# Average pooling over groups of four: rows of 126 KB per partition instead of blocks of 64 KB

## The chip, the cores and the metric

The kernel runs on one core of one Trainium2 chip. The metric is the device time of one execution in microseconds (us); lower is better. A core has compute engines with queues of their own (of these VectorE and ScalarE work here), SyncE, which only issues transfers, and 16 DMA engines that move all data between memory and the on-chip buffer of 128 partitions.

## The reference

The input is 64 x 256 x 8192 floats (536.87 MB), the output 64 x 256 x 2048 floats (134.22 MB). Each output is the mean of four neighbours, and the windows do not overlap:

```python
out_len = (length - kernel_size) // stride + 1     # kernel_size = stride = 4
for i in range(out_len):
    start = i * stride
    output[:, :, i] = np.mean(x[:, :, start : start + kernel_size], axis=2)
```

Since 8192 is a multiple of four, no window crosses the end of a row. So the input may be taken as one flat array, in which each four neighbours give one output, and cut anywhere at a multiple of four.

## The kernel before, in words

The flat input is cut into 64 blocks of 128 x 16,384 floats (8 MB). Within a block partition p holds the p-th run of 16,384 floats (64 KB), so a block is one contiguous piece of memory. The outputs of a block are 128 runs of 4096 floats (16 KB).

Every block goes through four steps. `load` (L44) is one DMA that SyncE issues, into one of two input buffers `xt` of 64 KB per partition. `sums` is two additions on VectorE: the first (L50) adds even and odd elements and writes the 8192 sums into the first half of the same input buffer, the second (L54) adds neighbours of these and writes 4096 sums into the result buffer `r`. `scale` (L59) multiplies by a quarter on ScalarE, in place in `r`. A store then writes the results to memory.

Results are gathered for two blocks (a group): `r` holds 2 x 4096 floats per partition and there are two such buffers. In the first four groups (`SINGLES` counts blocks here, 8) each block is scaled and stored by itself, from ScalarE's queue (L75, 2 MB). In the 26 groups after that the two blocks are scaled in one instruction and stored in one DMA (L78, 4 MB); in memory these are two runs of 16 KB per partition, 2 MB apart (`both`).

At the end stand block 62, loaded and stored alone, and block 63, loaded and computed in two pieces of 10,240 and 6144 floats per partition (`LAST`). The last whole group (blocks 60 and 61) is scaled after the loads of the end were issued, and it and all later results are stored from SyncE's queue (L87, L90, L95), behind the loads.

The order of the work follows from the queues and the buffers. SyncE issues the load of block i+2 once VectorE has finished both additions of block i, because they use the same input buffer. DMAs issued by SyncE go into one queue (q1 in the profile) and those of ScalarE into another (q10); the 16 DMA engines serve both. VectorE and ScalarE work in program order. VectorE's second addition needs a free result buffer, that is, the store of two groups earlier must have landed.

Of the kernel before, what the change touches and what calls it, by code (L numbers as in the profile page):

```python
# [1 line left out]

# [4 lines left out]


RUN = 16384

SINGLES = 8
LAST = (10240, 6144)


@with_exitstack
def kernel(
    ctx: ExitStack,
    tc: tile.TileContext,
    x: bass.AP,
    kernel_size: bass.AP,  # L20
    stride: bass.AP,
    out: bass.AP,
):
    nc = tc.nc
    K, S = int(kernel_size), int(stride)
    assert K == S == 4
    B, C, L = x.shape
    P = nc.NUM_PARTITIONS
    dt = x.dtype
    M = RUN // K  # L30
    blocks = B * C * L // (P * RUN)
    assert blocks * P * RUN == B * C * L and L % K == 0 and blocks % 2 == 0
    assert sum(LAST) == RUN

    xb = x.rearrange("b c l -> (b c l)").rearrange("(n p m) -> n p m", p=P, m=RUN)
    ob = out.rearrange("b c l -> (b c l)").rearrange("(n p m) -> n p m", p=P, m=M)

    pin = ctx.enter_context(tc.tile_pool(name="xin", bufs=2))
    pout = ctx.enter_context(tc.tile_pool(name="res", bufs=2))

    def load(i, a=0, b=RUN, xt=None):
        if xt is None:
            xt = pin.tile([P, RUN], dt, name="xt")
        nc.sync.dma_start(out=xt[:, a:b], in_=xb[i][:, a:b])  # L44
        return xt

    def sums(o, xt, a=0, b=RUN):
        v = xt[:, a:b].rearrange("p (m k) -> p m k", k=2)
        h = xt[:, a : (a + b) // 2]
        nc.vector.tensor_tensor(  # L50
            out=h, in0=v[:, :, 0], in1=v[:, :, 1], op=mybir.AluOpType.add
        )
        w = h.rearrange("p (m k) -> p m k", k=2)
        nc.vector.tensor_tensor(  # L54
            out=o, in0=w[:, :, 0], in1=w[:, :, 1], op=mybir.AluOpType.add
        )

    def scale(o):
        nc.scalar.mul(o, o, 1.0 / K)  # L59

    def edges(cuts):
        at = [sum(cuts[:j]) for j in range(len(cuts) + 1)]
        return list(zip(at[:-1], at[1:]))

    def both(i):
        return ob[i : i + 2].rearrange("n p m -> p n m")

    for i in range(0, blocks - 2, 2):
        r = pout.tile([P, 2, M], dt, name="r")
        for h in range(2):  # L70
            xt = load(i + h)
            sums(r[:, h, :], xt)
            if i < SINGLES:
                scale(r[:, h, :])
                nc.scalar.dma_start(out=ob[i + h], in_=r[:, h, :])  # L75
        if SINGLES <= i < blocks - 4:
            scale(r[:])
            nc.scalar.dma_start(out=both(i), in_=r[:])  # L78

    n = blocks - 1  # L80
    t = pout.tile([P, 2, M], dt, name="r")
    xt = load(n - 1)
    xl = None
    for a, b in edges(LAST):
        xl = load(n, a, b, xl)
    scale(r[:])
    nc.sync.dma_start(out=both(n - 3), in_=r[:])  # L87
    sums(t[:, 0, :], xt)
    scale(t[:, 0, :])
    nc.sync.dma_start(out=ob[n - 1], in_=t[:, 0, :])  # L90
    for a, b in edges(LAST):
        o = t[:, 1, a // K : b // K]
        sums(o, xl, a, b)
        scale(o)
        nc.sync.dma_start(out=ob[n][:, a // K : b // K], in_=o)  # L95


# [1 line left out]
_INS = ['x', 'kernel_size', 'stride']  # L99
_OUTS = [((64, 256, 2048), 'float32')]  # L100

_NUMBERS = {'kernel_size': 4, 'stride': 4}


# [26 lines left out]
```

## Time and profile before

| What | Value |
|---|---|
| median of 3 runs | 1554.46 us (1554.44 to 1555.88) |
| profiled execution: time | 1554.4 us |
| profiled execution: span | 1552.6 us |
| VectorE busy | 839.7 us (54%) |
| ScalarE busy | 227.4 us (15%) |
| DMA queues q1 and q10 | 81.1% and 18.9% of 16 engines' span |
| first addition, 128 x 8192 | 8692 ns each, 63 of them |
| second addition, 128 x 4096 | 4425 ns each, 63 of them |
| scale, 128 x 8192 and 128 x 4096 | 7029 ns and 3616 ns each |
| loads of 8 MB, issue to landing | 35.1 us (median of 63) |
| stores of 4 MB and 2 MB from ScalarE's queue, issue to landing | 52.0 us and 31.7 us (medians of 26 and 8) |

The span is the time from the first to the last record of the profiled execution; its full time is 1.8 us longer. Busy times are sums over instructions. The two queue rows count the time that packets took; a packet is the piece that one DMA engine moves at a time. A time from issue to landing contains the wait behind other packets of the same engines. The span is also shown in 40 equal slices, with the busy share of each engine in tenths (9 is 90% or more).

### The profile page before, as it was taken

What the parts mean: (1) busy time and instruction counts of PE and PEld (TensorE: products, weight loads), DVE (VectorE), ACT (ScalarE), POOL (GpSimd) and SP (SyncE); (2) the same over time, 40 slices, a digit from 0 to 9 for tenths busy, and PEclk for the clock granted to TensorE, in tenths of its full rate; (3) what the DMA queues carried; (4) which work ended last, traced back from release to release, by engine and by line L of the source; (5) the groups of instructions that cost most, each with busy time, mean ns of one, the idle gap of its engine ahead of it and who ended that gap; (6) DMA issues with size and microseconds to landing.
All of it is one profiled execution on the core that took longest, in us unless ns stands there. A gap on an engine that the chain in (4) does not pass through costs nothing.

```text
span 1552.6 us, 471 instructions
## 1 busy us (share of the span) xinstructions
DVE 839.7 (54%) x130; ACT 227.4 (15%) x39; POOL 0.2 (0%) x4
## 2 busy tenths in 40 slices
DVE  3646556546465464654646546455464554645646
ACT  1111101110111101111011110111101111011111
POOL 0000000000000000000000000000000000000000
DMA  9999999999999999999999999999999999999999
GB/s 417 420 434 438 439 439 439 412 445 444 413 433 435 443 438 439 432 424 429 439 438 433 437 434 419 439 432 438 439 419 434 434 437 439 441 423 442 422 440 400
DMA packets 18292, 671.12 MB, mean 432 GB/s; under 512 B 1649, under 2 KB 1649, under 8 KB 1777
## 3 DMA queue, kind: packets, MB, share of 16 engines
q1 hardware_dynamic: 10064, 545.26, 81.1%
q10 hardware_dynamic: 8224, 125.83, 18.9%
q14 instruction: 4, 0.02, 0.0%
HBM read 536.87 MB, written 134.22 MB: 432 GB/s over the span
## 4 chain that ended last, share of the span: by engine, by line
DMA 71%; DVE 28%; issue 0%; ACT 0%; DVEq 0%
DMA xt<-in_x_dram 71%; DVE xt L50 18%; DVE r L54 9%; ACT r L59 0%; DVEq L54 0%
## 5 line engine op out<-in xcount | busy, mean ns | idle before, releaser
L50 DVE TENSOR_TENSOR xt<-xt 128x8192 f32<-128x8192 f32 (+1 forms) x65 | 556.5, 8561 | 696.1 <-DMA xt<-in_x_dram 696.1
L59 ACT ACTIVATE r<-r 128x8192 f32<-128x8192 f32 (+3 forms) x38 | 226.2, 5951 | 1313.0 <-DVE r L54 1313.0
L54 DVE TENSOR_TENSOR r<-xt 128x4096 f32<-128x4096 f32 (+1 forms) x65 | 283.4, 4360 | 3.9
L59 ACT ACT_TABLE_LOAD x1 | 1.3, 1283 | 0.7 <-PEq L112 0.7
L112 POOL MEMSET const-bfloat16-1.0<- 128x1 bf16 x1 | 0.1, 101 | 0.0
L112 POOL MEMSET const-uint8-127<- 128x1 uint8 x1 | 0.1, 101 | 0.0
L112 POOL MEMSET const-float32-0.0<- 128x1 f32 x1 | 0.1, 98 | 0.2 <-issue 0.2
L112 POOL MEMSET const-float32-1.0<- 128x1 f32 x1 | 0.1, 98 | 0.0
## 6 DMA issues: line engine op xcount, KB each, us to landing
out_dram<-r ACTq DMA_DIRECT2D x26, 4096.0 KB, 52.0
out_dram<-r ACTq DMA_DIRECT2D x8, 2048.0 KB, 31.7
xt<-in_x_dram SPq DMA_DIRECT2D x1, 5120.0 KB, 23.1
out_dram<-r SPq DMA_DIRECT2D x1, 4096.0 KB, 33.0
xt<-in_x_dram SPq DMA_DIRECT2D x1, 3072.0 KB, 30.0
out_dram<-r SPq DMA_DIRECT2D x1, 2048.0 KB, 16.9
out_dram<-r SPq DMA_DIRECT2D x1, 1280.0 KB, 12.9
xt<-in_x_dram SPq DMA_DIRECT2D x63, 35.1
```

What stands on the lines that cost most here:

```text
L50: nc.vector.tensor_tensor(out=h, in0=v[:, :, 0], in1=v[:, :, 1], op=mybir.AluOpType.add)
L54: nc.vector.tensor_tensor(out=o, in0=w[:, :, 0], in1=w[:, :, 1], op=mybir.AluOpType.add)
L59: nc.scalar.mul(o, o, 1.0 / K)
L112: nc = _bacc.Bacc("TRN2", target_bir_lowering=False, num_devices=1)
```

## The change

The cut of the data changes. `RUN` becomes 16,128 floats (63 KB). A group of two halves is now one contiguous piece of memory in which partition p holds 2 x 16,128 floats (126 KB) in a row. The first half of each partition's run is one load and the second half another, so a load takes 63 KB per partition from rows that begin 126 KB apart. The results of a whole group are then one run of 2 x 4032 floats (31.5 KB) per partition.

There are 32 such groups. The first four (`SINGLES` counts groups now, 4) are scaled and stored in halves, 15.75 KB per partition, as before from ScalarE's queue; groups 4 to 30 are scaled and stored whole from ScalarE's queue; the last, group 31, is scaled in halves and stored whole from SyncE's queue. What is left is one contiguous block of 128 x 16,384 floats (`END`), which takes the place of the last block and is loaded, computed and stored in the same two pieces. The single block ahead of it is gone. Input buffers stay at 64 KB per partition; result buffers become 31.5 KB.

```diff
-RUN = 16384
+RUN = 16128
+END = 16384
 
-SINGLES = 8
+SINGLES = 4
 LAST = (10240, 6144)
...
-    xb = x.rearrange("b c l -> (b c l)").rearrange("(n p m) -> n p m", p=P, m=RUN)
-    ob = out.rearrange("b c l -> (b c l)").rearrange("(n p m) -> n p m", p=P, m=M)
+    xf = x.rearrange("b c l -> (b c l)")
+    of = out.rearrange("b c l -> (b c l)")
+    xb = xf[:body].rearrange("(n p h m) -> n p h m", p=P, h=2, m=RUN)
+    ob = of[: body // K].rearrange("(n p m) -> n p m", p=P, m=2 * M)
+    xe = xf[body:].rearrange("(p m) -> p m", p=P)
+    oe = of[body // K :].rearrange("(p m) -> p m", p=P)
...
-    for i in range(0, blocks - 2, 2):
-        r = pout.tile([P, 2, M], dt, name="r")
-        for h in range(2):
-            xt = load(i + h)
-            sums(r[:, h, :], xt)
-            if i < SINGLES:
-                scale(r[:, h, :])
-                nc.scalar.dma_start(out=ob[i + h], in_=r[:, h, :])
-        if SINGLES <= i < blocks - 4:
-            scale(r[:])
-            nc.scalar.dma_start(out=both(i), in_=r[:])
+    for g in range(groups):
+        r = pout.tile([P, 2 * M], dt, name="r")
+        for h in range(2):
+            xt = load(xb[g, :, h, :], 0, RUN)
+            o = r[:, h * M : (h + 1) * M]
+            sums(o, xt, 0, RUN)
+            if g < SINGLES or g == groups - 1:
+                scale(o)
+            if g < SINGLES:
+                nc.scalar.dma_start(out=ob[g][:, h * M : (h + 1) * M], in_=o)
+        if SINGLES <= g < groups - 1:
+            scale(r[:])
+            nc.scalar.dma_start(out=ob[g], in_=r[:])
...
-    n = blocks - 1
-    t = pout.tile([P, 2, M], dt, name="r")
-    xt = load(n - 1)
     xl = None
     for a, b in edges(LAST):
-        xl = load(n, a, b, xl)
-    scale(r[:])
-    nc.sync.dma_start(out=both(n - 3), in_=r[:])
-    sums(t[:, 0, :], xt)
-    scale(t[:, 0, :])
-    nc.sync.dma_start(out=ob[n - 1], in_=t[:, 0, :])
+        xl = load(xe, a, b, xl)
+    nc.sync.dma_start(out=ob[groups - 1], in_=r[:])
+    e = pout.tile([P, 2 * M], dt, name="r")
     for a, b in edges(LAST):
-        o = t[:, 1, a // K : b // K]
+        o = e[:, a // K : b // K]
         sums(o, xl, a, b)
         scale(o)
-        nc.sync.dma_start(out=ob[n][:, a // K : b // K], in_=o)
+        nc.sync.dma_start(out=oe[:, a // K : b // K], in_=o)
```

More of the change, by code (lines that the diff above doesn't have):

```diff
@@ L30, with load, sums @@
     M = RUN // K
-    blocks = B * C * L // (P * RUN)
-    assert blocks * P * RUN == B * C * L and L % K == 0 and blocks % 2 == 0
-    assert sum(LAST) == RUN
-    xb = x.rearrange("b c l -> (b c l)").rearrange("(n p m) -> n p m", p=P, m=RUN)
-    ob = out.rearrange("b c l -> (b c l)").rearrange("(n p m) -> n p m", p=P, m=M)
+    total = B * C * L
+    groups = total // (2 * P * RUN)
+    body = groups * 2 * P * RUN
+    assert L % K == 0 and total - body == P * END
+    assert sum(LAST) == END
+    xf = x.rearrange("b c l -> (b c l)")
[4 more added lines that the diff above has]
+    oe = of[body // K :].rearrange("(p m) -> p m", p=P)
     pin = ctx.enter_context(tc.tile_pool(name="xin", bufs=2))
     pout = ctx.enter_context(tc.tile_pool(name="res", bufs=2))
-    def load(i, a=0, b=RUN, xt=None):
+    def load(src, a, b, xt=None):
         if xt is None:
-            xt = pin.tile([P, RUN], dt, name="xt")
-        nc.sync.dma_start(out=xt[:, a:b], in_=xb[i][:, a:b])
+            xt = pin.tile([P, END], dt, name="xt")
+        nc.sync.dma_start(out=xt[:, a:b], in_=src[:, a:b])
         return xt
-    def sums(o, xt, a=0, b=RUN):
+    def sums(o, xt, a, b):
         v = xt[:, a:b].rearrange("p (m k) -> p m k", k=2)
@@ L63, in edges @@
         return list(zip(at[:-1], at[1:]))
-    def both(i):
-        return ob[i : i + 2].rearrange("n p m -> p n m")
-    for i in range(0, blocks - 2, 2):
-        r = pout.tile([P, 2, M], dt, name="r")
+    for g in range(groups):
+        r = pout.tile([P, 2 * M], dt, name="r")
         for h in range(2):
-            xt = load(i + h)
-            sums(r[:, h, :], xt)
-            if i < SINGLES:
-                scale(r[:, h, :])
-                nc.scalar.dma_start(out=ob[i + h], in_=r[:, h, :])
-        if SINGLES <= i < blocks - 4:
+            xt = load(xb[g, :, h, :], 0, RUN)
[6 more added lines that the diff above has]
+        if SINGLES <= g < groups - 1:
             scale(r[:])
-            nc.scalar.dma_start(out=both(i), in_=r[:])
-    n = blocks - 1
-    t = pout.tile([P, 2, M], dt, name="r")
-    xt = load(n - 1)
+            nc.scalar.dma_start(out=ob[g], in_=r[:])
     xl = None
     for a, b in edges(LAST):
-        xl = load(n, a, b, xl)
-    scale(r[:])
-    nc.sync.dma_start(out=both(n - 3), in_=r[:])
-    sums(t[:, 0, :], xt)
-    scale(t[:, 0, :])
-    nc.sync.dma_start(out=ob[n - 1], in_=t[:, 0, :])
+        xl = load(xe, a, b, xl)
+    nc.sync.dma_start(out=ob[groups - 1], in_=r[:])
+    e = pout.tile([P, 2 * M], dt, name="r")
     for a, b in edges(LAST):
-        o = t[:, 1, a // K : b // K]
+        o = e[:, a // K : b // K]
         sums(o, xl, a, b)
         scale(o)
-        nc.sync.dma_start(out=ob[n][:, a // K : b // K], in_=o)
+        nc.sync.dma_start(out=oe[:, a // K : b // K], in_=o)
 _INS = ['x', 'kernel_size', 'stride']
```

## The prediction

> **What bounds the kernel now.** I read the page from the top: engine shares, slices, queues, then the chain.
>
> ```profile
> span 1552.6 us, 471 instructions
> ...
> DVE 839.7 (54%) x130; ACT 227.4 (15%) x39; POOL 0.2 (0%) x4
> ...
> DMA  9999999999999999999999999999999999999999
> ...
> DMA packets 18292, 671.12 MB, mean 432 GB/s; under 512 B 1649, under 2 KB 1649, under 8 KB 1777
> ...
> q1 hardware_dynamic: 10064, 545.26, 81.1%
> q10 hardware_dynamic: 8224, 125.83, 18.9%
> ...
> DMA xt<-in_x_dram 71%; DVE xt L50 18%; DVE r L54 9%; ACT r L59 0%; DVEq L54 0%
> ```
>
> No compute engine is near full, but every slice of DMA is a 9, and the last two queue rows add to 100.0%: the packets of q1 (everything SP issues) and q10 (ScalarE's stores) fill 16 DMA engines for the whole span. The chain's 28% on VectorE does not contradict this. A load is issued when VectorE frees its buffer, so the chain goes through VectorE, but the engines work on the other buffer's load meanwhile. The windows, read stage by stage, say the same (columns: window, length, busy time with number of instructions for each engine, clock, DMA share, GB/s):
>
> ```profile
> 0.00:40.00 40.00, 13.12 (x2) 4.90 (x2) 0.20 (x4) 1.00 0.98 419
> ...
> 240.00:640.00 400.00, 218.79 (x34) 63.26 (x9) 0.00 (x0) 1.00 1.00 433
> ...
> 1040.00:1440.00 400.00, 212.46 (x33) 56.23 (x8) 0.00 (x0) 1.00 1.01 435
> ```
>
> The trace also records each DMA packet's start, size and duration. The first starts at 1.74 us, the last ends at 1551.4 us, and with sums of durations per size: a 65,536 B load packet 2418 ns (median), 40,960 B 1514, 24,576 B 912, a 16,384 B store packet 611, a 4 B semaphore packet 9. Two pieces of 40,960 and 24,576 B together take 2426 ns, 8 more than one of 65,536 B; four of 16,384 B take 2444, 26 more. So bytes cost 0.0367 ns each whatever the direction (1024 B are 37.6 ns), and a packet costs about 9 ns on top. But on each engine a packet starts 4 ns before the one ahead of it ends, load after store, store after load and load after load alike. What one more packet costs an engine is therefore about 5 ns, not 9. The whole follows: eight load and eight store packets make 8 x (2414 + 607) = 24.17 us, and in the steady part loads land every 24.18 us. Nothing but bytes and packets is in it.
>
> **Fewer packets, same bytes.** The load of a block stays one packet per partition; the store of a whole group becomes one packet of 32,256 B per partition instead of two of 16,384 B. Count before: loads 63 x 128 + 2 x 128 = 8320, stores 64 blocks x 128, with the last block in two, = 8320. After: loads 64 x 128 + 2 x 128 = 8448; stores four groups as halves 4 x 256 = 1024, 28 whole groups x 128 = 3584, the end in two 256, = 4864. That is 16,640 to 13,312, or 208 fewer per engine. Transfers go from 103 to 104, one 4 B packet more per engine (under 0.01 us). At 5 ns the 208 are 1.04 us; at the 9 ns of the bare durations 1.87 us. I take 1.0, since starts and not durations add up to the span, and keep 1.9 as an end of the range. All of it is on the path, since no engine has a pause to hide it in.
>
> **The order on the engines.** Store and load packets alternate one for one while a store is queued. Before, a 4 MB store has 16 packets per engine beside the 16 load packets of two blocks, so a store is nearly always there. After, it has 8: loads pass alone for about half the time. Packets of 63 KB cost 2376 ns from start to start and of 31.5 KB 1190, so a pair of blocks is 16 x 2376 + 8 x 1190 = 47.5 us, in place of 48.36, for 126/128 of the bytes. Within the pair the two loads become uneven, from 19.0 us (alone) to 28.5 (eight stores between). The short one needs cover: the next load is issued only when VectorE has done both additions of the block before. From the timeline, VectorE starts about 0.4 us after the last engine's semaphore packet, takes 8.69 + 4.43 us (x 63/64 after), and the first load of the kernel shows 1.0 us from issue to first packet: 14.5 us in all. Cover at the worst 19.0 - 14.5 = 4.5 us; the 16 engines' semaphore packets of one load lie at most 1.6 us apart. I cost it at nothing; if the cover were gone, each missing us would count up to 32 times. ScalarE's work goes from 7.03 to about 6.9 us per group and hides under the loads (it waits 41 us for VectorE each time). A result buffer is wanted again two groups later; stores land sooner than their 52 us, so this loosens.
>
> **The end.** Before, the last whole group was ready early, and a single block and a cut block followed. After, the store of the last group waits for the second half's sums and scale, while only the cut block's loads are queued ahead of it on SP:
>
> ```profile
> 1508.99 0.40 SPq L87 DMA_DIRECT2D out_dram<-r  x1
> ...
> 1521.90 4.43 DVE L54 TENSOR_TENSOR r<-xt 128x4096 f32<-128x4096 f32 x1
> 1526.24 5.48 DVE L50 TENSOR_TENSOR xt<-xt 128x5120 f32<-128x5120 f32 x1
> ...
> 1530.00 0.35 SPq L90 DMA_DIRECT2D out_dram<-r  x1
> ...
> 1536.98 4.54 SPq L95 DMA_DIRECT2D out_dram<-r  x2
> ```
>
> From the landing of the last 63 KB load: 0.4 + 13.0 (VectorE) + 3.6 (ScalarE, half a group) + 1.0 (issue to packet) = 18.0 us to the store's first packet. The cut block's loads need 8 x (1510 + 908) ns = 19.3 us alone, and the store of the group before, issued about 20 us after its own second load, still puts one or two packets of 1.19 us between: 20.5 to 21.7 us. Cover 2.5 to 3.7 us, so nothing lost. Behind it the queue holds 4 MB (about 9.5 us) while VectorE and ScalarE finish the cut block: the last piece of 0.75 MB can start at about 30.3 us after that landing and is due at 34. Before, SP's last issue began at 1541.2, 7 us before its turn. The end stays a full queue and 1.2 us after the last packet. If the first cover fails, the price is the gap, bounded by the 18.0 us chain less 16.0 if the cut loads ran 3 us ahead: 2 us; below zero it cannot go, since a full queue has no time to give.
>
> The fixed cost of one more transfer is zero by the rows (loads stacked in the queue land every 24.18 us, which the packets fill). The Trainium skill, "DMA: Bandwidth & Descriptors", section "Anatomy of one DMA", gives a transfer about 2.0 us fixed plus its bytes, and would speak against a 104th: by it the sum would be 1555.4. The trace disagrees for stacked transfers: 103 times 2 us on top of the bytes would already pass the span.
>
> **Spaced reads.** The trace of before shows no load whose rows lie apart in memory. Rows 126 KB apart instead of 64 KB may slow a packet or not. Nearest rows: packets of 65,536 B take 2415 ns at best, 2418 for nine in ten, 2439 at the 99th percentile; their excess over 2415 is 1.6 us per engine after the first 60 us. So this term lies between -1.6 us (all excess gone) and 512 x 21 ns = +10.8 us (every load packet like the slowest hundredth). I take zero: the time per byte is the same from 6 KB to 64 KB and for the stores' much shorter runs, so the memory's layout does not show in the engines' rate.
>
> **Sum.** The profiled execution took 1554.4 us (span 1552.6, 1.8 around it), the median of the runs is 1554.46, so they are the same. 1554.4 - 1.0 = **1553.4 us**, span 1551.6.
>
> **Rivals.** A measurement tells about 0.2% (3.1 us) from no change: faster is below 1551.4, slower above 1557.6.
>
> 1. Packets cost the full 9 ns and the excess vanishes: 1554.4 - 1.9 - 1.6 = 1550.9, faster. For it: the bare durations. Against: the 4 ns overlap is the same in every order of packets. 7%.
> 2. Spaced reads slow the load packets, slower: 512 per engine, so it decides against the change from 8 ns each (4.1 - 1.0 = 3.1 us). With 21 ns: 1554.4 + 10.8 - 1.0 = 1564.2. For it: nothing of the kind was run. Against: 0.0367 ns per byte at all sizes, as if the engine itself and not memory set it. 9%.
> 3. The change does not do what it says, and runs of 63 KB are cut. In two, 512 more packets per engine, 2.6 us: 1556.0; in four, 7.7 us: 1561.1. For: 63 KB is not a power of two. Against: 64 KB went as one packet. 4%, half of it slower.
> 4. A gap at the end or a transfer's fixed cost shows: 1553.4 + 2.0 = 1555.4. For: cover of some 2.5 us is thin. Against: the working above. 5%.
>
> The forecast itself has 75%. Faster 0.07, slower 0.09 + 0.02 = 0.11, same 0.82. The range, 1551.6 to 1556.6, holds the forecast with its ends (1552.5 at 9 ns, 1.4 us of spread between runs above), rival 4 and rival 3 in two pieces; outside lie rival 1 and most of 2.
>
> **What would show it.** Right: about 15,000 packets in the row (18,292 - 3328 + 16 = 14,980), queue rows still summing to 100%, DMA 9 in every slice, stores landing in 30 us instead of 52, VectorE's waits for loads alternating between some 7 and 13 us instead of 11, a span of 1551.6. Wrong: load packets above 2390 ns (rival 2), over 20,000 packets (rival 3), a slice below 9 near the end (rival 4), or a span under 1549.5 with packets below 2376 ns (rival 1).

## The result and the profile after

The changed kernel takes 1568.09 us (median of 4 runs, 1566.64 to 1568.16) against 1554.45 us before: 1.0085 times as long, 95% interval 1.0072 to 1.0097. The forecast was 1553.4 us, range 1551.6 to 1556.6. The profiled execution took 1568.07 us, its span 1566.3 us, which is 13.7 us more than before.

The page of the changed kernel, the rows that answer to those shown of before (engine shares, DMA slices, packets, queues, chain):

```profile
span 1566.3 us, 478 instructions
...
DVE 840.0 (54%) x132; ACT 227.6 (15%) x40; POOL 0.2 (0%) x4
...
DMA  9999999999999999999999999999999999999998
...
DMA packets 14979, 671.12 MB, mean 428 GB/s; under 512 B 1664, under 2 KB 1664, under 8 KB 1792
...
q1 hardware_dynamic: 9936, 543.10, 80.8%
q10 hardware_dynamic: 5040, 127.99, 18.9%
...
DMA xt<-in_x_dram 72%; DVE xt L57 18%; DVE r L61 9%; ACT r L66 0%; DVEq L61 0%
```

The packets fell as counted (14,979), the bytes are the same, the compute engines do the same work, and the two DMA queues still fill 99.7% of the span. But the mean rate fell from 432 to 428 GB/s. Engines that are always busy and move less are engines whose packets take longer. The windows say where (window, length, busy times with instruction counts, clock, DMA share, GB/s):

```profile
0.00:40.00 40.00, 12.92 (x2) 4.84 (x2) 0.20 (x4) 1.00 0.97 413
...
240.00:640.00 400.00, 217.43 (x35) 62.30 (x9) 0.00 (x0) 1.00 1.00 433
640.00:1040.00 400.00, 215.93 (x34) 55.38 (x8) 0.00 (x0) 1.00 1.00 428
1040.00:1440.00 400.00, 212.48 (x33) 55.38 (x8) 0.00 (x0) 1.00 1.00 429
1440.00:1566.00 126.00, 72.11 (x14) 24.79 (x6) 0.00 (x0) 1.00 0.96 411
```

Up to 640 us the rate is 433 GB/s, as before. Then it is 428 to 429 with the DMA share still 1.00, where the kernel before had

```profile
640.00:1040.00 400.00, 220.43 (x34) 56.23 (x8) 0.00 (x0) 1.00 1.00 432
```

and 435 after that. The last stretch has a share of 0.96: engines stand idle there.

The packet records of the trace settle the account. Below, *loss* is the time that load packets take above the usual duration of their size (2418 ns for 64 KB, 2380 ns for 63 KB), summed and divided by 16, so in us per engine. *Idle* is the time in which fewer than 16 engines had a packet, counted in the same way, from the start to the last packet.

| us per engine | before | after | difference |
|---|---|---|---|
| loss in load packets | 1.1 | 12.2 | +11.0 |
| idle while the end's stores are awaited | 0.1 | 1.4 | +1.4 |
| idle behind engines that end apart, rest | 0.7 | 2.9 | +2.1 |
| all else (bytes, number of packets) | 1547.8 | 1547.0 | -0.8 |
| from the first packet to the last | 1549.7 | 1563.4 | +13.7 |

So the gain that was forecast is there (0.8 us of the 1.0), and three losses cover it. The large one has a place. With the loads numbered from 0, a group's second load has an odd number. From load 11 on, where stores of whole groups run, the loss by the position of the packet within the load is:

```
second loads, packets 1 to 8:  0.96  0.12  1.98  6.37  0.73  0.02  0.05  0.02 us
first loads, all packets:      0.40 us
```

Most of it, 9.1 of 10.7 us, lies in the third to fifth packet of second loads. That is where the previous group's store, issued about 20 us after its second half landed, begins to send packets between the loads. It isn't there in every group: load 27 lost 0.78 us, 33 lost 1.06, 43 lost 0.09 and 55 lost 0.01, and from load 11 to load 21 none lost more than 0.03. The loss also varies from execution to execution: after the first 60 us it was 10.5, 10.8 and 12.3 us in three executions of this kernel (the two others stand among the experiments). Each loss below is read from one execution.

### The profile page after: what moved, and what is told of

Read it like the earlier page. It is cut to its first block, busy times and chain, and to the rows that moved or that the text cites. A ratio compares the mean times of both kernels' runs of the same rounds, so it can differ in the third digit from the quotient of the medians.

```text
span 1566.3 us, 478 instructions
## 1 busy us (share of the span) xinstructions
DVE 840.0 (54%) x132; ACT 227.6 (15%) x40; POOL 0.2 (0%) x4
## 2 busy tenths in 40 slices
DMA packets 14979, 671.12 MB, mean 428 GB/s; under 512 B 1664, under 2 KB 1664, under 8 KB 1792
## 4 chain that ended last, share of the span: by engine, by line
DMA 72%; DVE 27%; issue 0%; ACT 0%; DVEq 0%
DMA xt<-in_x_dram 72%; DVE xt L57 18%; DVE r L61 9%; ACT r L66 0%; DVEq L61 0%
## 5 line engine op out<-in xcount | busy, mean ns | idle before, releaser
L57 DVE TENSOR_TENSOR xt<-xt 128x8064 f32<-128x8064 f32 (+1 forms) x66 | 556.6, 8433 | 712.9 <-DMA xt<-in_x_dram 712.9
L66 ACT ACTIVATE r<-r 128x8064 f32<-128x8064 f32 (+3 forms) x39 | 226.3, 5804 | 1330.1 <-DVE r L61 1330.1
L61 DVE TENSOR_TENSOR r<-xt 128x4032 f32<-128x4032 f32 (+1 forms) x66 | 283.5, 4296 | 4.0
## 6 DMA issues: line engine op xcount, KB each, us to landing
out_dram<-r ACTq DMA_DIRECT2D x27, 4032.0 KB, 32.8
out_dram<-r SPq DMA_DIRECT2D x1, 4032.0 KB, 13.9
```

The lines of the kernel that those rows point to most:

```text
L57: nc.vector.tensor_tensor(out=h, in0=v[:, :, 0], in1=v[:, :, 1], op=mybir.AluOpType.add)
L61: nc.vector.tensor_tensor(out=o, in0=w[:, :, 0], in1=w[:, :, 1], op=mybir.AluOpType.add)
```

## The experiments

Four explanations of the loss were put to the test. **A**, changing turns: a store of eight packets leaves the loads alone half the time, and each change between loads alone and loads beside stores disturbs the engines. **B**, spaced rows: rows 126 KB apart slow the loads. **C**, long store packets: packets of 31.5 KB in place of 16 KB slow what runs beside them. **D**, both together: it is the joining of long store packets to loads that costs.

### Stores in halves throughout

```diff
-SINGLES = 4
+SINGLES = 31
```

> The changed kernel with every group but the last stored in halves (packets of 15.75 KB), so that a store packet stands beside every load packet from the first store to the end. Rows of loads and the end are as changed. In the changed kernel load packets of 63 KB lost 12.2 us per engine above their usual 2380 ns, nearly all in the third to fifth packet of a group's second load, where the store of the group before begins. Theory A, changing turns: loads alone and loads beside stores alternate in time, and each change puts the engines out of step; without the change of turns the loss falls under 2 us and the time to 1554 to 1557 us. Theory B, spaced rows: rows 126 KB apart slow the loads; the loss stays near 12 us and the time at 1566 to 1569. Theory C, long store packets: as A here, 1554 to 1557.

Measured: 1555.92 us, 1.0009 of before (0.9999 to 1.0019). The loss after 60 us is 0.3 us in place of 10.8. The windows of this kernel:

```profile
550.00:850.00 300.00, 161.52 (x26) 46.31 (x13) 0.00 (x0) 1.00 1.00 433
850.00:1150.00 300.00, 166.25 (x26) 42.75 (x12) 0.00 (x0) 1.00 1.00 434
1150.00:1450.00 300.00, 158.50 (x26) 46.31 (x13) 0.00 (x0) 1.00 1.00 434
```

The rows of the loads are as in the changed kernel, and the rate is that of before. B falls. A and C stand, since this edit shortens the packets and also fills the store queue.

### Contiguous loads

```diff
-    xb = xf[:body].rearrange("(n p h m) -> n p h m", p=P, h=2, m=RUN)
+    xb = xf[:body].rearrange("(n h p m) -> n p h m", p=P, h=2, m=RUN)
```

> The changed kernel with each load reading one contiguous piece of memory (rows of 63 KB directly one behind the other). Each half then gets other rows than its place in the output would need; all sizes, counts and stores are as changed. Theory A (changing turns) and theory C (long store packets): nothing changes, 1565 to 1569 us and about 12 us of lost time per engine in the load packets. Theory B (spaced rows): the loss is gone, 1553 to 1556 us.

Measured: 1567.34 us, 1.0082 of before (1.0067 to 1.0097), a loss of 12.3 us in the same packets (7.2 us in the fourth of second loads).

```profile
550.00:850.00 300.00, 158.39 (x25) 41.53 (x6) 0.00 (x0) 1.00 1.00 429
850.00:1150.00 300.00, 159.31 (x25) 41.53 (x6) 0.00 (x0) 1.00 1.01 431
1150.00:1450.00 300.00, 163.62 (x26) 44.09 (x7) 0.00 (x0) 1.00 1.00 429
```

Taking the spacing away changes neither the time nor the loss by more than executions of one kernel differ. B falls a second time, from the other side.

### The kernel before with long stores

```diff
     def both(i):
-        return ob[i : i + 2].rearrange("n p m -> p n m")
+        return ob[i : i + 2].rearrange("n p m -> (n p m)").rearrange("(p m) -> p m", m=2 * M)
...
-            nc.scalar.dma_start(out=both(i), in_=r[:])
+            nc.scalar.dma_start(out=both(i), in_=r[:].rearrange("p n m -> p (n m)"))
```

The last group's store is changed in the same way.

> The kernel before, with the store of a whole group written as one run of 32 KB per partition (two blocks' results side by side in the group's 4 MB, not where they belong). Contiguous loads of 64 KB and the end stay. Theories A and C: the load packets lose some 8 to 14 us per engine where stores begin, 1561 to 1568 us. Theory B: no loss, 1553 to 1554.5 us.

Measured: 1566.83 us, 1.0078 of before (1.0063 to 1.0093), a loss of 12.5 us. With the stores alone changed, the kernel before gets nearly the whole of the 13.7 us.

```profile
250.00:550.00 300.00, 159.19 (x25) 48.13 (x7) 0.00 (x0) 1.00 1.00 431
550.00:850.00 300.00, 164.31 (x25) 42.17 (x6) 0.00 (x0) 1.00 1.00 430
850.00:1150.00 300.00, 161.85 (x26) 42.17 (x6) 0.00 (x0) 1.00 1.00 429
1150.00:1450.00 300.00, 157.42 (x24) 42.17 (x6) 0.00 (x0) 1.00 1.00 428
```

### The changed kernel once more

> The changed kernel as it is, once more with a profile. If the loss depends on addresses and a fixed order, the same loads lose the same time (most in the loads numbered 27, 33, 35, 41, 47 and 51, nearly none in 43, 55, 57 and 61) and the time is 1566 to 1568 us; if it comes from chance on the engines, other loads lose.

Measured: 1569.67 us and a loss of 13.9 us, again in the third and fourth packet of second loads. But other loads lose: load 27 only 0.05 us, 55 now 0.85, and loads 15 and 17 already 0.4 each. The place within the load is fixed, the load is not, so the addresses that the program names don't decide which loads lose.

### Short packets, changing turns

```diff
-            nc.scalar.dma_start(out=both(i), in_=r[:])
+            nc.scalar.dma_start(out=ob[i], in_=r[:, 0, :])
```

> The kernel before with contiguous loads of 64 KB and store packets of 16 KB, but of each group stored whole only the first block's results are written (2 MB in place of 4; the others are left out). So store packets are short, and the store queue is empty for about half of each pair of blocks. Read by what the load packets lose above their usual 2418 ns. Theory A (changing turns): 6 to 14 us per engine in the load packets, where stores begin. Theory C (long store packets): under 2 us. The time is some 1425 to 1445 us for want of 54 MB of stores.

Measured: 1428.62 us and a loss after 60 us of 0.4 us. The store queue is empty half the time here, and nothing is lost. Theory A by itself falls.

### Long packets, no change of turns

```diff
-        for h in range(2):
-            xt = load(xb[g, :, h, :], 0, RUN)
+        xt = load(xb[g, :, 0, :], 0, RUN)
+        for h in range(2):
             o = r[:, h * M : (h + 1) * M]
-            sums(o, xt, 0, RUN)
+            if h == 0:
+                sums(o, xt, 0, RUN)
+            else:
+                again(o, xt, 0, RUN)
```

`again` is the second addition alone.

> The changed kernel with the second load of each group left out (both halves of the results come from the first half's sums). So eight load packets of 63 KB and eight store packets of 31.5 KB stand in each group, and once stores have begun a store is nearly always queued beside a load. Read by what the load packets lose above 2380 ns. Theory A: under 2 us per engine. Theory C: as much for each group as in the changed kernel, some 6 to 14 us. The time is some 915 to 980 us with half of the loads.

Measured: 954.47 us. The loss after 60 us is 2.9 us, of which 2.65 fall before 250 us, while the first groups' stores still hold up the loads. Of this, 1.5 us lie in one load, which begins at 190.6 us after a pause of the loads: 0.8 in its first packets and 0.8 in its fourth, where a long store issued at 196.56 us joins. In the 700 us after 250 us, loads land every 28.5 us with a store packet beside each load packet, and the loss is 0.26 us. Long packets that are always there cost nothing, so theory C by itself falls as well. With the two before it, this leaves D: long store packets that *join*.

### Stores in the loads' queue

```diff
             xt = load(xb[g, :, h, :], 0, RUN)
+            if h == 1 and done is not None:
+                nc.sync.dma_start(out=ob[g - 1], in_=done[:])
...
-            nc.scalar.dma_start(out=ob[g], in_=r[:])
+        done = r
```

The first four groups are stored whole too.

> The changed kernel with all stores in the loads' own queue: SyncE issues the store of a group right behind the second load of the next group, and every group is stored whole (31.5 KB packets). Loads and stores change turns just as often, and rows and sizes are as changed, but every engine changes at the same packet, because there is one order for all. Theory A in its narrower form (it is the differing points of change on the 16 engines that costs): no loss, end not late, 1552.8 to 1554.0 us. Theory A in its wider form (any change between loads alone and stores) and theory C: 5 to 12 us lost, 1558 to 1566.

Measured: 1558.11 us, 1.0021 of before (1.0012 to 1.003). The time lies at the lower end of the second range, but the loss, 2.7 us after 60 us (1.3 of it before 250 us), lies in neither. With one order for all engines nothing can join at differing packets, and some three quarters of the loss are gone. The edit changes a second thing: behind the loads in one queue, store packets no longer alternate with load packets, so it doesn't tell which of the two took the loss away. What keeps the kernel slower is that the engines end apart: the first are done with their loads 4.6 us before the last, and at the end 2.9 us per engine are idle. The Trainium skill ("DMA: Bandwidth & Descriptors", section "Issuing engines are not separate DMA queues") holds that DMAs of different issuing engines share the 16 DMA engines and that spreading them saves only issue time. They do share the engines, but which queue the stores went through changed the loss from 10.8 to 2.7 us, so here the order in which packets met on them counted, not issue time alone.

### Half stores with another end

```diff
-            if g < SINGLES:
+            if g < SINGLES or h == 0:
                 nc.scalar.dma_start(out=ob[g][:, h * M : (h + 1) * M], in_=o)
...
-    nc.sync.dma_start(out=ob[groups - 1], in_=r[:])
+    nc.sync.dma_start(out=ob[groups - 1][:, M:], in_=r[:, M:])
```

`SINGLES` is 31 as in the first experiment.

> The changed kernel with all groups stored in halves, the last group too: its first half from ScalarE's queue as soon as it is scaled, its second half from SyncE behind the cut block's loads. With all groups but the last in halves the time was 1555.9 us, and the store of the last group began 1 to 2 us after the cut block's loads had ended. If that pause is what remains against the kernel before, it goes here and the time is 1554.0 to 1554.9 us; if the order of the end is of no account, 1555.5 to 1556.3.

Measured: 1557.58 us, 1.7 us more than without this edit. The expectation was wrong. The first pause is closed, but now only 2 MB instead of 4 stand behind the cut block's loads, and they are gone before the cut block's results are ready. The packet records show 1.6 us per engine idle ahead of the 1.25 MB store and 1.1 ahead of the last. What the end needs is enough stored bytes in the queue, not only an early first one.

### An earlier join

```diff
-            if g < SINGLES or g == groups - 1:
-                scale(o)
+            scale(o)
+            if h == 0 and g > SINGLES:
+                nc.scalar.dma_start(out=ob[g - 1], in_=done[:])
...
-            scale(r[:])
-            nc.scalar.dma_start(out=ob[g], in_=r[:])
+        done = r
```

> The changed kernel with each whole group's store issued some 16 us later (behind the scaling of the next group's first half, on ScalarE's queue; all groups are scaled in halves). Packets, rows and the number of joins are as changed. Theory D: the loss arises where long store packets join the loads, so it moves with the join, from the third to fifth packet of a group's second load to its last two packets and the first four of the load after it; its sum stays at 6 to 14 us per engine and the time at 1560 to 1570 us. Rival: the place is set by something else at that point of the load (VectorE's start, rows of memory); then the loss stays in the third to fifth packet of the second load.

The edit did not do what its expectation says. The store came out ahead of the next group's scaling, so it is issued not later but earlier, because only half a group's scaling now stands between. The timelines of the changed kernel and of this one, at the same group:

```profile
384.71 4.36 DVE L61 TENSOR_TENSOR r<-xt 128x4032 f32<-128x4032 f32 x1
...
389.10 6.92 ACT L66 ACTIVATE r<-r 128x8064 f32<-128x8064 f32 x1 [40.96 <-DVE r L61]
396.05 0.34 ACTq L84 DMA_DIRECT2D out_dram<-r  x1
```

```profile
385.63 4.36 DVE L61 TENSOR_TENSOR r<-xt 128x4032 f32<-128x4032 f32 x1
...
390.02 3.56 ACT L66 ACTIVATE r<-r 128x4032 f32<-128x4032 f32 x1 [25.57 <-DVE r L61]
393.62 0.34 ACTq L80 DMA_DIRECT2D out_dram<-r  x1
```

From the second addition to the issue it is 11.3 us in the first and 8.0 us in the second, 3.4 us or 1.4 load packets less. Measured: 1570.86 us and a loss of 17.1 us, by position in second loads

```
1.27  7.51  5.61  0.35  0.09  0.07  0.07  0.10 us
```

The loss has moved from the third and fourth packet to the second and third, about as far as the join has. It belongs to the join, not to a place in the load. It also sets in earlier: load 15 loses 0.65 us already, where in the changed kernel none of loads 11 to 21 lost more than 0.03.

### How long a store packet must be

```diff
-            nc.scalar.dma_start(out=both(i), in_=r[:].rearrange("p n m -> p (n m)"))
+            nc.scalar.dma_start(out=both(i)[:, :6144], in_=r[:].rearrange("p n m -> p (n m)")[:, :6144])
```

The edit is to the kernel before with long stores; 6144 floats are 24 KB, and the other two have 7168 (28 KB) and 7680 (30 KB).

> The kernel before with stores of whole groups as runs of 24 KB per partition (the last quarter of each group's results is left out, the rest lies side by side, not where it belongs). Eight store packets for sixteen load packets, as with 16 KB (loss 0.4 us after 60 us) and 32 KB (11.3 us). If the length of the packet that joins decides: a loss between, 2 to 9 us. If it is a threshold, near one of the ends. The time is some 1492 us plus the loss, for want of 27 MB.

> The kernel before with stores of whole groups as runs of 28 KB per partition (the last eighth of each group's results is left out, the rest lies side by side, not where it belongs). With 16, 24 and 32 KB the load packets lost 0.4, 0.5 and 11.3 us after 60 us. By degrees between 24 and 32 KB: 2 to 9 us; a threshold above 24 KB: near 0.5 or near 11. The time is some 1523 us plus the loss.

> The kernel before with stores of whole groups as runs of 30 KB per partition (the last sixteenth of each group's results is left out, the rest lies side by side, not where it belongs). If the ratio of two to the 64 KB loads decides: a loss of 0.5 to 3 us. If the length decides with its threshold near 30 KB: more than 6 us or again about 0.5, which by itself would tell nothing apart. The time is some 1539 us plus the loss.

| store packet | loss after 60 us | time |
|---|---|---|
| 16 KB (611 ns) | 0.4 us | 1428.6 us, fewer bytes |
| 24 KB (912 ns) | 0.5 us | 1491.8 us, fewer bytes |
| 28 KB (1062 ns) | 0.6 us | 1524.1 us, fewer bytes |
| 30 KB (1138 ns) | 8.5 us | 1549.2 us, fewer bytes |
| 32 KB (1213 ns) | 11.3 us | 1566.8 us |

The 16 KB row is the kernel of "Short packets, changing turns". Beside loads of 64 KB there is a step between 28 and 30 KB, not a slope.

### Length or ratio

In both lossy kernels a store packet lasted half as long as a load packet. The changed kernel with

```diff
-RUN = 16128
+RUN = 14336
```

keeps that ratio with store packets of 28 KB.

> The changed kernel with RUN = 14336: loads of 56 KB per partition from rows 112 KB apart, whole-group stores of 28 KB, 36 groups, the same contiguous last block. A store packet is half a load packet, as in the changed kernel, but 28 KB long. If the ratio of two decides (engines then meet again and again at the same offsets): a loss of 7 to 14 us in the load packets and 1564 to 1572 us. If the length decides (28 KB lost 0.6 us beside loads of 64 KB): under 2 us of loss and 1555 to 1558 us.

Measured: 1556.95 us, 1.0018 of before (1.0009 to 1.0028), a loss of 1.0 us after 60 us. (One of its ten executions took 1562.64 us; no trace shows why.) A store packet takes 1062 ns and a load packet 2116 ns, again twice as long, and the loss is gone. So the ratio doesn't decide. The length of the store packet would explain every row, but so would the length of the pair: all kernels that lost had store packets of 30 KB or more beside load packets of 63 KB or more, and no run has long store packets that join short load packets.

```profile
550.00:850.00 300.00, 165.09 (x29) 43.24 (x7) 0.00 (x0) 1.00 1.00 433
850.00:1150.00 300.00, 165.02 (x30) 43.24 (x7) 0.00 (x0) 1.00 1.00 434
1150.00:1450.00 300.00, 161.89 (x29) 46.40 (x8) 0.00 (x0) 1.00 1.00 434
```

### Engines that begin again together

```diff
+        if g >= 8 and g % 4 == 0:
+            rest = pin.tile([P, END], dt, name="xt")
+            nc.gpsimd.memset(rest[:, :8], 0.0)
```

> The changed kernel in which, at every fourth group from the ninth, the next load is held back until both input buffers have been summed, so that the load queue runs dry and all engines begin again together (six times, 6 to 15 us each, so the time is 1600 to 1660 us). Read by what the load packets lose after 60 us, each held-back load's first packet left out. Theory D with engines out of step as a condition: the loss builds up only over some six groups, so it stays under 4 us in place of 10.8. Rival, long packets that join are enough by themselves: 8 us or more.

This edit held no load back; VectorE's waits for loads are those of the changed kernel (712.6 us in all, 712.9 there). So it is in effect one more execution of that kernel: 1567.47 us, a loss after 60 us of 10.5 us. The next edit was to make the load wait for data:

```diff
+        if behind is not None:
+            nc.vector.tensor_copy(out=xt[:, :8], in_=behind)
         nc.sync.dma_start(out=xt[:, a:b], in_=src[:, a:b])
...
+            hold = g >= 6 and g % 3 == 0 and h == 0
+            xt = load(xb[g, :, h, :], 0, RUN, behind=done[:, 2 * M - 8 :] if hold else None)
```

> The changed kernel in which, at groups 6, 9, 12 and so on to 30, the first load waits for a copy (VectorE, 8 elements) of the group before's scaled results, so that the load queue runs dry nine times and all engines begin again together. Each hold costs 10 to 22 us; the time is 1650 to 1770 us. Read by what the load packets lose after 60 us, the first packet of each held load left out. If engines out of step are a condition: under 4 us in place of 10.8, since the loss has not come up by the third join after a common start. If long packets that join are enough: 8 us or more.

Measured: 1701.52 us. The timeline at one of the nine holds:

```profile
452.25 43.56 SPq L53 DMA_DIRECT2D xt<-in_x_dram  x3
452.25 6.92 ACT L68 ACTIVATE r<-r 128x8064 f32<-128x8064 f32 x1 [41.07 <-DVE r L63]
459.21 0.34 ACTq L88 DMA_DIRECT2D out_dram<-r  x1
459.21 0.17 DVE L52 COPY xt<-r 128x8 f32<-128x8 f32 x1 [6.99 <-ACT r L68]
482.50 8.56 DVE L59 TENSOR_TENSOR xt<-xt 128x8064 f32<-128x8064 f32 x1 [23.12 <-DMA xt<-in_x_dram]
```

The held load is issued at 452.25 us, when VectorE has finished the group before; the copy at 459.21 us holds back only the load after it. That was enough for the load queue to run dry: the held load's first packets begin together, at 453.2 to 453.6 us. The store is issued at 459.21 us, and the load's fourth packets begin at 461.0 us. By position, the nine held loads lost, on average,

```
0.79  0.00  0.02  0.80  0.00  0.00  0.00  0.00 us
```

and all other loads after load 10 together 0.5 us. The loss in the first packets is that of the common start, since no store packet is near. The loss in the fourth packets is that of the join. Without the first packets the loss is 8.0 us, just inside the second range of the expectation: engines that have run out of step for long are not a condition. But the 18 joins that came later, in loads that were not held, lost 0.03 us each on average, where the changed kernel lost 0.4 at a join. So a long join costs 0.8 us when the engines began together 8 us earlier, next to nothing at the next two, and in the changed kernel at most 0.03 us at its first six and more after that. What tells a costly join from a free one stays open.

### Half stores and the end as before

```diff
+    xt = load(xe, 0, END)
+    sums(e[:, : END // K], xt, 0, END)
...
-    for g in range(groups):
+    for g in range(groups - 1):
...
+    xt = load(xb[n, :, 0, :], 0, RUN)
     for a, b in edges(LAST):
-        xl = load(xe, a, b, xl)
-    nc.sync.dma_start(out=ob[groups - 1], in_=r[:])
+        xl = load(xb[n, :, 1, :], a, b, xl)
+    scale(r[:])
+    nc.sync.dma_start(out=ob[n - 1], in_=r[:])
```

> The changed cut (spaced rows of 63 KB, half-group stores of 15.75 KB) with the end as before: the contiguous block of 64 KB rows comes first, the last group is loaded whole and then in two pieces, and the group ahead of it is scaled late and stored behind the loads. If the 1.4 us that the kernel with half-group stores still takes above the kernel before are the pause at the end and engines that end apart: 1554.0 to 1554.9 us. If spaced rows or 63 KB cost anything by themselves: 1555.4 or more.

Measured: 1555.75 us, 1.0007 of before (0.9998 to 1.0016). By the letter the second case, but the records leave little for the rows: of 1.2 us more between the first packet and the last than before, 0.8 are idle time at the very end (1.5 us per engine in place of 0.7, one engine being a us behind), 0.1 are load packets, and some 0.2 are its 36 more packets per engine at 5 ns each. There is no pause. Its interval does not tell it from the kernel before; no kernel of this study that moves all the bytes took less time than that one.

## Why the prediction was wrong, step by step

**What bounds the kernel**: right. Every experiment's time moved with the DMA engines' packets and pauses; VectorE counted only where an edit let the loads wait for it.

**Fewer packets, same bytes**: right, 14,979 packets for a count of 14,980, and 0.8 us gained for 1.0.

**The order on the engines**: this step failed. Its picture of the order was right. Where nothing is lost, the first loads of two groups land 47.57 us apart on the engine that is done first (298.17 to 345.74 us), for 47.5; VectorE's waits alternate between 7.3 and 14.9 us for 7 and 13; stores land in 32.8 us for 30. What failed is the price: the step took packets to last in the new order what they lasted in the old one, start to start, and so costed the change of order at nothing. In the trace of before, store packets of 16 KB were nearly always queued, so no row showed a long packet joining loads that run alone. That operation had no bound; only the cover of VectorE's wait was priced, and that cover held. It costs 11.0 us, some 0.4 us on average at each of 27 joins.

**The end**: the working was right up to the queue. The store's first packet came 17.8 us after the landing of the last 63 KB load (1529.8 to 1547.6 us) for 18.0. The cover was counted from the wrong engine: the landing is that of the last engine, and the first ones were 7 us ahead, since the lost time falls unevenly on the engines. They had finished the cut block's loads from 1545.6 us on and stood until 1547.6:

```profile
1530.19 8.56 DVE L57 TENSOR_TENSOR xt<-xt 128x8064 f32<-128x8064 f32 x1 [14.88 <-DMA xt<-in_x_dram]
1538.78 4.36 DVE L61 TENSOR_TENSOR r<-xt 128x4032 f32<-128x4032 f32 x1
1543.17 3.56 ACT L66 ACTIVATE r<-r 128x4032 f32<-128x4032 f32 x1 [24.27 <-DVE r L61]
...
1546.76 0.35 SPq L89 DMA_DIRECT2D out_dram<-r  x1
```

The last of these lines is SyncE's issue of the last group's store, right behind ScalarE's scaling. The pause is 1.4 us per engine, inside the 2 us that the prediction gave it at most; rival 4 was that mechanism, and it had 5%. Its sign is there too: the last slice of DMA is an 8. By itself it would have kept the time within the range.

**A transfer's fixed cost**: right to leave at zero; nothing of 2 us per transfer shows in a full queue. What the Trainium skill says in the cited section ("DMA: Bandwidth & Descriptors", "Anatomy of one DMA") is measured on transfers that GpSimd issues; those of both kernels are issued by SyncE and ScalarE.

**Spaced reads**: taken at zero, and zero is what contiguous and spaced rows show between them (a loss of 12.3 and 12.2 us). Yet this step's rival came nearest the time. Rival 2 foresaw load packets slowed by more than 8 ns each and a time of 1564.2 us, and load packets did rise to a mean of 2404 ns from 2380. The symptom was right and the cause was not: it is not the rows that are read but the packets that join. More weight on rival 2 would have come nearer by luck, not by insight.

**The range** took in the costs that had been named. A re-ordering of packets on shared engines was not among them, so it had no bound to bring in.

## What to carry to other kernels

When every engine is busy all the time and the kernel still gets slower, look at the durations of single packets by place, not at shares. Merging short runs into longer ones isn't free because bytes and packet counts say so: if the longer packets leave a queue empty in between, they have to join again, and here a join of packets of 31.5 KB cost 0.4 us per engine on average, against 5 ns saved per packet. Here that means: eight packets fewer per engine and group saved 0.04 us, and the join that came with them cost ten times as much. With the new cut, a small store beside every load (1555.92 us) was better than half as many large ones (1568.09 us); and at an end whose cover is counted in single us, count it from the fastest engine.

## What the hardware showed that was not expected

- Load packets of 63 and 64 KB are slowed where store packets of 30 KB or more from another queue join them after a pause (8.5 to 15.5 us per engine in a kernel, after its first 60 us), and not with 28 KB or less (at most 1.0 us), whether the load packet is 2.0 or 2.3 times as long. Whether it is the store packet's length or that of the pair is not shown. With the same long packets always queued the loss was 0.26 us in 700 us.
- The packets that lose begin before the first store packet has a record: at 638.3 us, load packets of 2489 to 3486 ns, with the store issued at 636.08 us and the first store packet at 639.7 us, the next at 641.0. Why is open; no run looks inside an engine.
- Engines that begin together after a pause lose 0.6 to 0.9 us in their first load packet (nine holds in one kernel, and 0.7 to 0.9 at the start of every kernel).
- Time lost by one engine is not made up: each engine has the same number of packets, so a single packet of 2951 ns in the kernel before left its engine behind until the end (1.0 us there, up to 7 us in the changed kernel). That packet began at 560.0 us, right after a packet of 8 KB of the instruction queue (q14) at 559.7 us. Three such packets in the changed kernel can't make the losses at 27 joins.
